# Global attention of a two-layer hybrid block: wider steps for the row maxima, single banks for the scores, values in larger pieces, and another order around them

## The chip, the core and the metric

The kernel runs on one core of a Trainium2 chip. A core has five engines with a queue each: TensorE (PE, matrix products), VectorE (DVE), ScalarE (ACT), GpSimd (POOL) and SyncE (SP, which here only starts DMAs). Each queue takes its instructions in order, and an instruction that waits holds back those behind it. The metric is the device time of one execution in microseconds (us). The profile is one execution taken by the hardware profiler; its times count from the first instruction of the span.

## What is computed

A stack of two layers works on 1024 latent tokens and 256 context tokens of width 1024. Cut to what matters here:

```python
for l in range(2):
    h  = rms_norm(x, norm_gain[l]) * (1 + scale) + shift          # also for ctx
    aq, ak, av, ag, bz, bg, nq, nk, nv, ng = split(h @ w_in[l])
    # global attention: 8 query heads, 2 key heads (4 query heads share one), head size 64
    aq, ak = rope_2d(rms_norm(aq)) * 64**-0.5, rope_2d(rms_norm(ak))
    a_out  = softmax(aq @ concat(ak, ak_ctx).T) @ concat(av, av_ctx)   # 1024 x 1280 per head
    b_out  = pool_branch(bz)                                        # mean windows
    n_out  = neighbourhood_attn(nq, nk, nv, rpb)                    # 8 x 16 windows, plus ctx
    y = concat(a_out * silu(ag), b_out * silu(bg), n_out * silu(ng)) @ w_out[l]
    x = x + gate * y
```

Every value is float32. Where the kernel needs a matrix product of that precision at a higher rate, it splits an operand into a rounded high part and the rest (`hh` and `hl`) and adds the products.

## The kernel before, in words

A layer has the stages input projection, neighbourhood attention (for the first layer also attention of the context tokens over themselves), global attention, and output projection. This change is about the global attention and about the neighbourhood stage ahead of it, in which the first steps of the global attention are hidden.

The **global attention** is cut into eight *units* (`ga_unit`): half of the latent tokens (512 columns, `cc`), one key head `g`, and a pair of query heads, which the code counts with `hi` 0 and 1. In a unit the 1280 keys are taken in five *fifths* (`kp` 0 to 4) of 256 keys. For each fifth and head:

- `scores`: four matmuls of 512 columns on PE into a pair of PSUM banks (1024 columns, `ps_w`, there are two pairs), then one ACT exponential of 1024 columns into a probability buffer `gp` (pool `prob`, seven buffers).
- the sum over keys: the probability tiles of the fifths are added up elementwise in `gacc`, on POOL for fifths 1 to 3 (lines 1037 and 1040) and on DVE for fifth 4, after which DVE folds it to 512 columns (line 1042).
- `values`: the product with the value vectors (line 1049), four matmuls into `ps_c`. It stands one fifth behind the scores.

When a unit is through, ACT copies the product to SBUF (`gosb`), and `finish` follows in the middle of the next unit: PE sums `gacc` over the partitions (line 1058), ACT takes logarithm and exponential (`gr`) for the reciprocal, DVE refines it, POOL multiplies the product with the loaded gate (`ggate`, line 1067), DVE multiplies the two, and `store_u` writes the rounded part (`hh`, ACT) and the rest (`hl`, DVE).

A softmax needs the **maximum of each row** first. `shift` gets it in 20 steps for each unit: PE multiplies 128 queries by 512 keys into one of the three single banks `ps_b` (lines 1003 and 1008), and DVE reduces the bank (`gmx`, lines 1004 and 1009). A 21st step, `shift_rows`, transposes the maxima on PE, ACT copies them (`gmr`), and two small DMAs write them as a row into `q2`, by which the scores come out with the maximum already taken off. These steps run ahead of their unit: 161 closures stand in one list, `shifts`, and `shift_step(n)` takes n of them at each place. Before the first unit starts, 21 + `GA_AHEAD` = 29 of them are to be through; they run in the last 10 (second layer: 7) blocks of the neighbourhood stage, three to a block (one after head 0, two after head 1), what is left at its end.

The **neighbourhood stage** takes 128 queries at a time (`pair_unit`), here called a *block*: two heads, each with scores in a pair of banks, exponential, transposes of the probabilities in two of the three single banks, and the product with the values. The first layer has 28 blocks (20 and 8 of the context), the second 16. What must be loaded or computed early is hung on the block's number with `early(i, fn)`.

PE's order is as the code is written. The order on the other engines is made by the framework's planner, which places each instruction by its own estimate of when it is ready; SP's order too. The order that came out is fixed in the program: the engines don't change it when they run.

Of the kernel before, what the change touches and what calls it, by code (L numbers as in the profile page):

```python
# [31 lines left out]
GA_AHEAD = 8  # L32
# [42 lines left out]
def hybrid_block_kernel(  # L75
# [298 lines left out]
    for l in range(DEPTH):  # L374
# [532 lines left out]
        def early(i, fn):  # L907
            before.setdefault(max(i, 0), []).append(fn)

        order = [0, 1, 6, 7, 4, 5, 2, 3] + list(range(NTL, ntq))  # L910
        for pr in range(2):
# [13 lines left out]
            else:  # L925
                early(s0 + 4, lambda: gk(0))
# [48 lines left out]
        def ga_unit(cc, g, pr):  # L975
# [16 lines left out]
            def shift(i):  # L992

                hi, j = divmod(i, 10)
                if i == 0:
                    load2()
                    st.mx = small.tile([P, 2, 4, 3], F32, tag="gmx", name="gmx")
                q1, mx = st.q1[hi], st.mx[:, hi]
                k1 = gk(g)[0]
                S = ps_one("ps_m")  # L1000
                if j < 8:
                    qt, half = divmod(j, 2)
                    PE.matmul(S, q1[:, qt * P:(qt + 1) * P], k1[:, half * 512:(half + 1) * 512], start=True, stop=True)  # L1003
                    DVE.reduce_max(out=mx[:, qt, half:half + 1], in_=S, axis=AX.X)  # L1004
                    return
                q0 = 2 * (j - 8)
                for i in range(2):
                    PE.matmul(S[:, i * 256:(i + 1) * 256], q1[:, (q0 + i) * P:(q0 + i + 1) * P], k1[:, SEQ:NT], start=True, stop=True)
                DVE.reduce_max(out=mx[:, q0:q0 + 2, 2], in_=S.rearrange("p (a b) -> p a b", a=2), axis=AX.X)
                if hi and j == 9:  # L1010
                    st.nn = small.tile([P, 8], F32, tag="gnn", name="gnn")
                    DVE.tensor_reduce(out=st.nn, in_=st.mx.rearrange("p h q k -> p (h q) k"), op=ALU.max, axis=AX.X, negate=True)
# [11 lines left out]
            def scores(hi, kp):  # L1024
                k1, k2 = gk(g)
                S = ps_pair("ps_st").rearrange("p (a b) -> p a b", a=2)
                for i in range(2):
                    kc = slice((2 * kp + i) * P, (2 * kp + i + 1) * P)
                    PE.matmul(S[:, i, :], k1[:, kc], st.q1[hi], start=True, stop=False)  # L1029
                    PE.matmul(S[:, i, :], k2[:, kc], st.q2[hi], start=False, stop=True)  # L1030
                p = ap_.tile([P, 2, 512], F32, name="gp", tag="prob", bufs=PB)
                ACT.activation(out=p, in_=S, func=AF.Exp)  # L1032
                st.p[hi, kp] = p
                pf = p.rearrange("p a b -> p (a b)")
                if kp == 1:
                    st.acc[hi] = ap_.tile([P, 1024], F32, name="gacc", tag="prob", bufs=PB)
                    POOL.tensor_tensor(out=st.acc[hi], in0=st.p[hi, 0].rearrange("p a b -> p (a b)"), in1=pf, op=ALU.add)  # L1037
                elif kp > 1:
                    eng = DVE if kp == 4 else POOL
                    eng.tensor_tensor(out=st.acc[hi], in0=st.acc[hi], in1=pf, op=ALU.add)  # L1040
# [13 lines left out]

            def finish():
                s_ps = ps_one("ps_gs")
                for hi in range(2):
                    PE.matmul(s_ps[hi * 64:(hi + 1) * 64, :], ones, st.acc[hi][:, 0:512], start=True, stop=True)
                gt = ap_.tile([P, 512], F32, name="ggate", tag="fin", bufs=4)
                SP.dma_start(out=gt, in_=agd[f, :, cs])  # L1060
                r0 = ap_.tile([P, 512], F32, name="gr0", tag="fin", bufs=4)
                ACT.activation(out=r0, in_=s_ps, func=AF.Ln)
                ACT.activation(out=r0, in_=r0, func=AF.Exp, scale=-1.0)
# [3 lines left out]
                POOL.tensor_tensor(out=gt, in0=gt, in1=st.osb, op=ALU.mult)
# [28 lines left out]
        n_shifts = 7 if last else 10  # L1096
        n_ahead = 21 + GA_AHEAD
# [6 lines left out]
        n_all = len(shifts)  # L1104
        for n, u in enumerate(units + [None, None]):
# [4 lines left out]
            for hi in range(2):  # L1110
# [16 lines left out]
        shift_step(n_ahead - (n_all - len(shifts)))  # L1127
# [30 lines left out]
        gunits[-1][2](4, 0)  # L1158
        gunits[-1][2](4, 1)
# [176 lines left out]
```

## Time and profile before

| | |
|---|---|
| median of 3 runs | 1539.0 us (1536.47 to 1542.13) |
| the profiled execution | 1539.72 us, span 1537.9 us |
| granted TensorE clock, mean | 0.996 |
| busy share of the span | PE 96%, DVE 56%, ACT 41%, POOL 33% |
| neighbourhood stage, layer 0 and 1 | about 391 to 513 us, and 1134 to 1227 us |
| global attention, layer 0 and 1 | 513.26 to 730.27 us, and 1226.7 to 1443.74 us |

The page gives for each engine the time in which it was busy, and for groups of like instructions the line, the operation, the output and input tiles, the shapes, the count, the busy time, the mean duration and the idle time of the engine ahead of them with what ended it. In the order of time, a row gives the start, the duration, the engine, the line, the operation, the tiles, the count, and in brackets the idle time ahead of it and what ended it. PE's matmuls overlap: the start of the next row, not the duration, tells how long one holds the engine. A matmul of float32 (line 1049, 1058) shows as two records.

### The profile page before, as it was taken

The page shows a single profiled execution, that of the slowest core. Times are in us where ns is not written, and L with a number is a line of the kernel's source. Part 1 is how long each engine was busy: PE and PEld are TensorE (multiplying, and loading weights), DVE is VectorE, ACT ScalarE, POOL GpSimd, SP SyncE. Part 2 cuts the span into 40 slices and gives each one's busy share as a digit, 9 for nine tenths or more (in the row PEclk, how much of TensorE's full clock was granted, in tenths as well). Part 3 has the DMA queues.
Part 4 walks back from the last instruction along what each step waited for, and adds up shares of the span by engine and source line. Part 5 has one row for each costly group of instructions (what it writes and reads, how often), then busy time and mean ns, then how long its engine had stood idle before and what let it go on. Part 6 is the DMA issues. An engine that isn't in the chain of part 4 may idle for free.

```text
span 1537.9 us, 22259 instructions
## 1 busy us (share of the span) xinstructions
PE 1474.2 (96%) x8001; PEld 1072.8 (70%) x8001; DVE 860.2 (56%) x1666; ACT 637.6 (41%) x1220; POOL 513.1 (33%) x630
## 2 busy tenths in 40 slices
PE   5999999999999999998999999999998999999999
PEld 3787777788888555553788888878787854544577
DVE  3645234552678678875533543464358868786522
ACT  4543132333676444444312452332466544444400
POOL 0232336000134556565001233460013265565300
PEclk9999999999999999999999999999999999999999
DMA  9436455537745200101413222243697301001331
GB/s 317 140 97 219 133 158 162 165 107 192 178 113 159 73 27 25 39 8 55 168 58 109 76 93 91 85 142 82 155 227 172 89 21 42 21 24 39 133 121 55
DMA packets 153039, 167.91 MB, mean 109 GB/s; under 512 B 35384, under 2 KB 112032, under 8 KB 152864
## 3 DMA queue, kind: packets, MB, share of 16 engines
q1 hardware_dynamic: 152928, 166.48, 37.0%
q8 instruction: 63, 1.03, 0.3%
q14 instruction: 48, 0.39, 0.1%
HBM read 126.45 MB, written 40.86 MB: 109 GB/s over the span
## 4 chain that ended last, share of the span: by engine, by line
PE 80%; DVE 8%; ACT 4%; DMA 3%; issue 3%; SPq 1%; POOL 0%; DVEq 0%; POOLq 0%; ACTq 0%
PE ps_w L418 8%; PE ps_w L419 8%; PE ps_w L420 8%; PE ps_c L1049 8%; PE ps_w L1204 4%; PE ps_w L1207 4%; PE ps_w L1205 4%; PE ps_w L1029 4%; PE ps_b L1003 4%; PE ps_w L1030 3%; PE ps_c L894 3%; PE ps_b L882 2%; PE ps_w L426 2%; PE ps_w L428 2%; PE ps_w L427 2%
## 5 line engine op out<-in xcount | busy, mean ns | idle before, releaser
L1032 ACT ACTIVATE gp<-ps_w 128x1024 f32<-128x1024 f32 x160 | 162.4, 1022 | 190.9 <-PE ps_w L1030 155.3
L418 PE MATMUL ps_w<-wh,hh 128*128 128x512 f32 (+1 forms) x624 | 235.7, 378 | 2.2 <-ACT wh L287 2.2
L419 PE MATMUL ps_w<-wl,hh 128*128 128x512 f32 (+1 forms) x624 | 229.0, 367 | 1.0 <-DVE wl L288 1.0
L420 PE MATMUL ps_w<-wh,hl 128*128 128x512 f32 (+1 forms) x624 | 228.4, 366 | 0.0
L1004 DVE TENSOR_REDUCE gmx<-ps_b 128x1 f32<-128x512 f32 x256 | 171.7, 685 | 73.2 <-PE ps_b L1003 69.0
L1049 PE MATMUL ps_c<-gp,av 128*64 128x512 f32 x640 | 165.0, 609 | 10.3 <-ACT gp L1032 10.3
L1040 POOL TENSOR_TENSOR gacc<-gacc,gp 128x1024 f32<-128x1024 f32 x64 | 161.4, 2548 | 25.8 <-ACT gp L1032 25.5
L418 PEld LDWEIGHTS ps_w<-wh,hh 128*128 128x128 f32 x624 | 118.4, 190 | 27.8 <-issue 4.0
L419 PEld LDWEIGHTS ps_w<-wl,hh 128*128 128x128 f32 x624 | 117.8, 189 | 21.3 <-DVE wl L288 2.2
L420 PEld LDWEIGHTS ps_w<-wh,hl 128*128 128x128 f32 x624 | 117.6, 188 | 21.3
L1030 PE MATMUL ps_w<-gq,kst 128*128 128x512 f32 x320 | 126.7, 396 | 0.0
L1204 PE MATMUL ps_w<-woh,hh 128*128 128x512 f32 x272 | 109.5, 403 | 0.0
L1205 PE MATMUL ps_w<-wol,hh 128*128 128x512 f32 x272 | 107.4, 395 | 0.0
L639 DVE TENSOR_REDUCE qss<-sq 128x8 f32<-128x512 f32 (+2 forms) x58 | 31.1, 537 | 135.7 <-ACT sq L637 135.7
L1049 PEld LDWEIGHTS ps_c<-gp,av 128*64 128x64 f32 x640 | 42.5, 136 | 87.3 <-issue 65.2
L1037 POOL TENSOR_TENSOR gacc<-gp 128x1024 f32<-128x1024 f32 x32 | 75.8, 2369 | 50.0 <-ACT gp L1032 50.0
L288 DVE TENSOR_TENSOR wl<-wraw,wh 128x512 fp32r<-128x512 f32 (+1 forms) x96 | 66.3, 707 | 38.8 <-ACT wh L287 37.4
L1207 PE MATMUL ps_w<-woh,hl 128*128 128x512 f32 x272 | 85.6, 395 | 0.0
L426 PE MATMUL ps_w<-hh,wh 128*128 128x512 f32 (+1 forms) x208 | 81.6, 392 | 2.4 <-ACT wh L287 2.4
L866 ACT ACTIVATE prob<-ps_w,m 128x768 f32<-128x768 f32 (+2 forms) x88 | 72.7, 826 | 19.4 <-DVE m L853 7.4
L428 PE MATMUL ps_w<-hh,wl 128*128 128x512 f32 (+1 forms) x208 | 79.6, 382 | 0.0
L427 PE MATMUL ps_w<-hl,wh 128*128 128x512 f32 (+1 forms) x208 | 79.2, 381 | 0.0
(225 smaller groups left out, 2916.2 us busy)
## 6 DMA issues: line engine op xcount, KB each, us to landing
wmod<-in_w_mod_dram SPq DMA_DIRECT2D x48, 512.0 KB
wraw<-in_w_in_dram SPq DMA_DIRECT2D x64, 256.0 KB
gq<-qad SPq DMA_DIRECT2D x64, 128.0 KB
woraw<-in_w_out_dram SPq DMA_DIRECT2D x14, 512.0 KB
wraw<-in_w_in_dram SPq DMA_DIRECT2D x48, 128.0 KB
kst<-knd SPq DMA_DIRECT2D x16, 320.0 KB
qad<-qkhi SPq DMA_DIRECT2D x18, 256.0 KB
qad<-qklo SPq DMA_DIRECT2D x18, 256.0 KB
```

Of the source, the lines that this page charges most:

```text
L418: PE.matmul(ps[:, :n], a, wh[:, off:off + n], start=(k == 0), stop=False)
L419: PE.matmul(ps[:, :n], a, wl[:, off:off + n], start=False, stop=False)
L420: PE.matmul(ps[:, :n], b, wh[:, off:off + n], start=False, stop=(k == KT - 1))
L426: PE.matmul(ps[:, :n], wh[:, fs], hh[:, k, ts_], start=(k == 0), stop=False)
L1004: DVE.reduce_max(out=mx[:, qt, half:half + 1], in_=S, axis=AX.X)
L1030: PE.matmul(S[:, i, :], k2[:, kc], st.q2[hi], start=False, stop=True)
L1032: ACT.activation(out=p, in_=S, func=AF.Exp)
L1040: eng.tensor_tensor(out=st.acc[hi], in0=st.acc[hi], in1=pf, op=ALU.add)
L1049: PE.matmul(st.o[hi * 64:(hi + 1) * 64, :], av[:, kt, g * 64:(g + 1) * 64], st.p[hi, kp][:, i, :], start=(kt == 0), stop=(kt == NTT - 1))
L1204: PE.matmul(ps[:, i2, :], a, oh[:, cs], start=(k == 0), stop=False)
L1205: PE.matmul(ps[:, i2, :], a, ol[:, cs], start=False, stop=False)
L1207: PE.matmul(ps[:, i2, :], b, oh[:, i2 * 512:(i2 + 1) * 512], start=False, stop=(k == KT - 1))
```

## The change

- **Maxima.** For the first unit and for head 0 of the second the steps stay as they were (20 and 10 steps, single banks `ps_b`). For all others a step (`shift2`) covers 1024 columns in a pair of banks `ps_w`: 5 steps for a head, each with two matmuls of 512 columns (or four of 256) and one DVE reduction of 1024. The negated maximum is taken for each head by itself (`shift_head`).
- **Scores** go to the three single banks `ps_b`, with one exponential of 512 columns for each bank: two for a fifth and head in place of one.
- **Values** are taken two fifths at a time, at fifth 2 and fifth 4; the last fifth comes at fifth 1 of the next unit, and right behind it the sums (`sums`) and `finish`.
- **The sum over keys** lies in memory of its own (the neighbourhood's values `nv`, and two key buffers), no longer in the ring of probability buffers. In the last unit, head 0's additions run on DVE.
- **Finish.** ACT copies the sums to SBUF; the last product runs on POOL, and ACT's rounded part (`Identity`, line 1095) and DVE's rest (line 1096) are taken from it.
- **Steps ahead.** `GA_AHEAD` is 31 and counts all of them: 30 steps of the old kind and one transpose are through before the first unit; they run in the last 16 blocks of the neighbourhood stage, one after each head. The loads of the first two units' queries and of the first key head move up to the block ahead of that; in the second layer, with 16 blocks, to block 0. In the stage itself there are three steps at a unit's first fifth and two at each of the others.

Three places on which the change acts, in the order in which each engine's instructions stand. The names carry buffer numbers, to tell buffers of one kind apart.

**ACT in unit 1 of layer 0, around the sums of unit 0.** Before; `gp_5981` belongs to head 1 of fifth 2, `gp_6010` and `gp_6032` to the two heads of fifth 3:

```order
L1032 ACTIVATE gp_5981<-ps_w1_3846 128x1024
L1062 ACTIVATE gr0_5996<-ps_b1_70 128x512
L1063 ACTIVATE gr0_5996<-gr0_5996 128x512
L1032 ACTIVATE gp_6010<-ps_w0_3845 128x1024
L1032 ACTIVATE gp_6032<-ps_w1_3846 128x1024
L815 ACTIVATE hh_95<-gt1_5999 128x512
L1019 ACTIVATE gmr_6036<-ps_b1_70 8x128
```

After; `gp_5971` belongs to head 1 of fifth 1, `gp_5985` and `gp_6006` to the two heads of fifth 2:

```order
L1074 ACTIVATE gosb_5954<-ps_c_72 128x512
L1081 ACTIVATE gr0_5958<-ps_b0_69 128x512
L1082 ACTIVATE gt1_5959<-ps_b0_69 128x512
L1088 ACTIVATE gr0_5958<-gr0_5958 128x512
L1053 ACTIVATE gp_5971<-ps_b1_70 128x512
L1053 ACTIVATE gp_5971<-ps_b2_71 128x512
L1053 ACTIVATE gp_5985<-ps_b0_69 128x512
L1053 ACTIVATE gp_5985<-ps_b1_70 128x512
L1095 ACTIVATE hh_95<-ggate_5962 128x512
L1053 ACTIVATE gp_6006<-ps_b2_71 128x512
L1053 ACTIVATE gp_6006<-ps_b0_69 128x512
```

The rounded part for `hh` stands four exponentials of 512 columns behind the sums, with the exponentials of head 1 of fifth 2 right behind it; before, it stood two of 1024 behind.

**POOL in the same unit.** Before:

```order
L1067 TENSOR_TENSOR ggate_5994<-ggate_5994,gosb_5919 128x512
L1037 TENSOR_TENSOR gacc_5940<-gp_5910,gp_5938 128x1024
L1037 TENSOR_TENSOR gacc_5956<-gp_5928,gp_5954 128x1024
L1040 TENSOR_TENSOR gacc_5940<-gacc_5940,gp_5966 128x1024
L1040 TENSOR_TENSOR gacc_5956<-gacc_5956,gp_5981 128x1024
```

After:

```order
L1058 TENSOR_TENSOR gacc_5755<-gp_5910,gp_5939 128x1024
L1058 TENSOR_TENSOR gacc_5756<-gp_5926,gp_5971 128x1024
L1091 TENSOR_TENSOR ggate_5962<-ggate_5962,gosb_5954 128x512
L1061 TENSOR_TENSOR gacc_5755<-gacc_5755,gp_5985 128x1024
L1093 TENSOR_TENSOR ggate_5962<-ggate_5962,gt1_5959 128x512
L1061 TENSOR_TENSOR gacc_5756<-gacc_5756,gp_6006 128x1024
```

Before, the product with the gate stood ahead of the unit's additions; now it stands between them, and the second product (line 1093), which writes what `hh` is taken from, stands behind the addition for head 0 of fifth 2.

**PE at the start of layer 1's neighbourhood stage.** `kst_10615` is the rounded part of key head 0 of the global attention. Before:

```order
L428 MATMUL ps_c_72<-hh_95,wl_10257 128x512
L846 MATMUL ps_w0_10531<-kst_10348,nq_10360 128x256
L847 MATMUL ps_w0_10531<-kst_10349,nq_10360 128x256
...
L882 MATMUL ps_b1_70<-ident_85,prob_10593 128x128 x4
```

After:

```order
L428 MATMUL ps_c_72<-hh_95,wl_10274 128x512
L1001 MATMUL ps_b1_70<-kst_10615,hh_95 128x512
L1001 MATMUL ps_b2_71<-kst_10615,hh_95 128x512
L846 MATMUL ps_w1_10549<-kst_10365,nq_10377 128x256
L847 MATMUL ps_w1_10549<-kst_10366,nq_10377 128x256
...
L882 MATMUL ps_b0_69<-ident_85,prob_10625 128x128 x4
```

The first two steps of the maxima stand between the last matmul of the gate projection and the first scores of the stage. On SP, the key head's load stands behind the loads of two units' queries:

```order
L372 DMA hh_95<-qad_77 64x512 x2
L730 DMA agd_81<-gate_10537 128x512
L372 DMA hl_96<-qad_77 64x512 x2
L372 DMA hh_95<-qad_77 64x512 x2
L372 DMA hl_96<-qad_77 64x512 x2
L755 DMA kst_10615<-kad_78 64x1280 x2
```

Before, three loads of queries stood there; the other five came later in the stage's first blocks, and the key head's load was hung on block 12 of 16.

The diff, cut to its core:

```diff
-GA_AHEAD = 8
+GA_AHEAD = 31
...
-                early(s0 + 4, lambda: gk(0))
+                pass
...
+            def shift_head(hi, n):
+                DVE.tensor_reduce(out=st.nn[:, 4 * hi:4 * hi + 4], in_=st.mx[:, hi, :, 0:n], op=ALU.max, axis=AX.X, negate=True)
...
+            def shift2(hi, j):
+                if j == 0:
+                    (load2 if hi else shift_new)()
+                S = ps_pair("ps_m")
+                if j < 4:
+                    for half in range(2):
+                        shift_mm(hi, S, j, half * 512, half * 512, 512)
+                    DVE.reduce_max(out=st.mx[:, hi, j, 0:1], in_=S, axis=AX.X)
+                    return
+                for qt in range(4):
+                    shift_mm(hi, S, qt, qt * 256, SEQ, 256)
+                DVE.reduce_max(out=st.mx[:, hi, :, 1], in_=S.rearrange("p (a b) -> p a b", a=4), axis=AX.X)
+                shift_head(hi, 2)
...
             def scores(hi, kp):
                 k1, k2 = gk(g)
-                S = ps_pair("ps_st").rearrange("p (a b) -> p a b", a=2)
+                p = ap_.tile([P, 2, 512], F32, name="gp", tag="prob", bufs=PB)
                 for i in range(2):
+                    S = ps_one("ps_st")
                     kc = slice((2 * kp + i) * P, (2 * kp + i + 1) * P)
...
-                p = ap_.tile([P, 2, 512], F32, name="gp", tag="prob", bufs=PB)
-                ACT.activation(out=p, in_=S, func=AF.Exp)
+                    PE.matmul(S, k1[:, kc], st.q1[hi], start=True, stop=False)
+                    PE.matmul(S, k2[:, kc], st.q2[hi], start=False, stop=True)
+                    ACT.activation(out=p[:, i, :], in_=S, func=AF.Exp)
...
-                    st.acc[hi] = ap_.tile([P, 1024], F32, name="gacc", tag="prob", bufs=PB)
+                    st.acc[hi] = accs[n % 2][hi]
...
-                    eng = DVE if kp == 4 else POOL
+                    eng = DVE if kp == 4 or (n == 7 and hi == 0) else POOL
...
+            def sums():
+                S = ps_one("ps_gs")
+                for hi in range(2):
+                    PE.matmul(S[hi * 64:(hi + 1) * 64, :], ones, st.acc[hi][:, 0:512], start=True, stop=True)
...
+                ACT.activation(out=st.r0, in_=S, func=AF.Ln)
+                ACT.activation(out=st.t1, in_=S, func=AF.Copy)
+
             def finish():
...
-                DVE.tensor_tensor(out=t1, in0=s_ps, in1=r0, op=ALU.mult)
+                DVE.tensor_tensor(out=t1, in0=t1, in1=r0, op=ALU.mult)
                 DVE.scalar_tensor_tensor(out=t1, in0=t1, scalar=-2.0, in1=r0, op0=ALU.add, op1=ALU.mult)
                 POOL.tensor_tensor(out=gt, in0=gt, in1=st.osb, op=ALU.mult)
-                DVE.scalar_tensor_tensor(out=t1, in0=t1, scalar=-1.0, in1=gt, op0=ALU.mult, op1=ALU.mult)
-                store_u(f, cc * 512, 512, t1)
...
+                POOL.tensor_tensor(out=gt, in0=gt, in1=t1, op=ALU.mult)
+                hi, lo = hh[:, f, cs], hl[:, f, cs]
+                ACT.activation(out=hi, in_=gt, func=AF.Identity, scale=-1.0)
+                DVE.scalar_tensor_tensor(out=lo, in0=gt, scalar=-1.0, in1=hi.bitcast(F32), op0=ALU.mult, op1=ALU.subtract)
...
+                way, k = (0, 10) if i + hi < 2 and i < 2 else (6, 5)
...
+        n_shifts = min(len(units), (GA_AHEAD + 1) // 2)
         for i in range(2):
-            early(len(units) - 12, gunits[i][4])
+            early(len(units) - n_shifts - 1, gunits[i][4])
+        early(len(units) - n_shifts, lambda: gk(0))
...
-                if hi == 0 and n >= nun - n_shifts:
-                    shift_step(1, n_all - n_ahead)
-            shift_step(2 if n >= nun - n_shifts else 0, n_all - n_ahead)
+                if n >= nun - n_shifts:
+                    shift_step(1, n_least)
...
             for kp in range(5):
-                lagv = None
-                if kp:
-                    lagv = lambda h, kp=kp: values(kp - 1, h)
-                elif pv:
-                    lagv = lambda h: pv[2](4, h)
                 scores(0, kp)
                 shift_step(1)
-                if lagv:
-                    lagv(0)
-                    lagv(1)
-                shift_step(2 if kp == 4 else 1)
+
+                if kp == 1 and pv:
+                    pv[2](4, 0)
+                    pv[2](4, 1)
+                    pv[7]()
+                    pv[3]()
+                elif kp in (2, 4):
+                    for j in range(4):
+                        values(kp - 2 + j // 2, j % 2)
                 scores(1, kp)
-                shift_step(2)
-                if kp == 2 and pv:
-                    pv[3]()
+                shift_step(2 if kp == 0 else 1)
```

In these loops `u[4]` is `load`, `pv[7]` is `sums`, `pv[3]` is `finish`, and `way` 0 and 6 are `shift` and `shift2`.

More of the change, by code (lines that the diff above doesn't have):

```diff
@@ L990, in load2, with shift_new, shift_mm, shift @@
                     load_parts(st.q2[hi], qad, 2 * f + hi, cs)
[L992 to L999, printed above, removed]
+            def shift_new():
+                st.mx = small.tile([P, 2, 4, 3], F32, tag="gmx", name="gmx")
+                st.nn = small.tile([P, 8], F32, tag="gnn", name="gnn")
+            def shift_head(hi, n):
+                DVE.tensor_reduce(out=st.nn[:, 4 * hi:4 * hi + 4], in_=st.mx[:, hi, :, 0:n], op=ALU.max, axis=AX.X, negate=True)
+            def shift_mm(hi, S, qt, o, k0, n):
+                PE.matmul(S[:, o:o + n], st.q1[hi][:, qt * P:(qt + 1) * P], gk(g)[0][:, k0:k0 + n], start=True, stop=True)
+            def shift(hi, j):
+                if j == 0:
+                    (load2 if hi else shift_new)()
                 S = ps_one("ps_m")
@@ L1002, in shift @@
                     qt, half = divmod(j, 2)
-                    PE.matmul(S, q1[:, qt * P:(qt + 1) * P], k1[:, half * 512:(half + 1) * 512], start=True, stop=True)
-                    DVE.reduce_max(out=mx[:, qt, half:half + 1], in_=S, axis=AX.X)
+                    shift_mm(hi, S, qt, 0, half * 512, 512)
+                    DVE.reduce_max(out=st.mx[:, hi, qt, half:half + 1], in_=S, axis=AX.X)
                     return
@@ L1007, in shift @@
                 for i in range(2):
[L1008 to L1012, printed above, removed]
+                    shift_mm(hi, S, q0 + i, i * 256, SEQ, 256)
+                DVE.reduce_max(out=st.mx[:, hi, q0:q0 + 2, 2], in_=S.rearrange("p (a b) -> p a b", a=2), axis=AX.X)
+                if j == 9:
+                    shift_head(hi, 3)
+            def shift2(hi, j):
+                if j == 0:
+                    (load2 if hi else shift_new)()
+                S = ps_pair("ps_m")
[8 more added lines that the diff above has]
+                shift_head(hi, 2)
             def shift_rows():
@@ L1055, in finish @@
             def finish():
-                s_ps = ps_one("ps_gs")
-                for hi in range(2):
-                    PE.matmul(s_ps[hi * 64:(hi + 1) * 64, :], ones, st.acc[hi][:, 0:512], start=True, stop=True)
                 gt = ap_.tile([P, 512], F32, name="ggate", tag="fin", bufs=4)
                 SP.dma_start(out=gt, in_=agd[f, :, cs])
-                r0 = ap_.tile([P, 512], F32, name="gr0", tag="fin", bufs=4)
-                ACT.activation(out=r0, in_=s_ps, func=AF.Ln)
+                r0, t1 = st.r0, st.t1
@@ L1075, in hybrid_block_kernel @@
+            return shift, scores, values, finish, load, shift_rows, shift2, sums
+        gunits = [ga_unit(4 * cc + 2 * g + pr, cc, g, pr) for cc in range(2) for g in range(2) for pr in range(2)]
         shifts = []
         for i, u in enumerate(gunits):
-            own = [lambda u=u, j=j: u[0](j) for j in range(20)]
+            own = []
+            for hi in range(2):
+                way, k = (0, 10) if i + hi < 2 and i < 2 else (6, 5)
+                own += [lambda u=u, way=way, hi=hi, j=j: u[way](hi, j) for j in range(k)]
@@ L1136, in hybrid_block_kernel @@
         nu = len(gunits)
+        nvf = nv.rearrange("p t c -> p (t c)")
+        accs = [[nvf[:, 0:1024], nvf[:, 1024:2048]],
+                [ak_.tile([P, NT], F32, name="gacc", tag="kst", bufs=6)[:, 0:1024] for _ in range(2)]]
         for i in range(nu):
-            _, scores, values, finish, _, _ = gunits[i]
+            _, scores, values, finish = gunits[i][:4]
             pv = gunits[i - 1] if i else None
```

18 lines of the change are left out of this document (6 added, 12 removed).

## Prediction

> **What bounds the kernel now.** I read the chain of waits first. Its first line says that four fifths of the time to the end hang on PE. The table of windows with the two global attention stages comes next (the last three columns are PE's granted clock, the DMA share and GB/s), and then PE's waits in the first stage (us in total, times, longest).
>
> ```profile
> PE 80%; DVE 8%; ACT 4%; DMA 3%; issue 3%; SPq 1%; POOL 0%; DVEq 0%; POOLq 0%; ACTq 0%
> 513.26:730.27 217.01, 205.37 (x841) 106.82 (x840) 156.12 (x200) 98.68 (x116) 128.86 (x59) 0.99 0.10 30
> 1226.70:1443.74 217.04, 205.46 (x840) 106.72 (x839) 157.03 (x201) 98.70 (x116) 128.80 (x58) 0.99 0.10 31
> PE ps_b L1003 <- DVE gmx L1004: 6.4, 6, 1.2
> PE ps_c L1049 <- ACT gp L1032: 5.1, 3, 3.1
> ```
>
> The stages are alike, so one is worked out and doubled. PE (first pair) is busy 205 of 217 us; DVE, ACT and POOL have 60 to 118 us of slack each, but POOL's 129 us come in few, long pieces. PE waits 11.5 us in nine places. That is the most that better timing alone can win in a layer.
>
> Then PE's order of time for a steady unit, with the starts of units 4 and 6 (617.48, 671.71), the end of 6 and the end of 7:
>
> ```profile
> 605.05 1.08 PE L1058 MATMUL ps_b<-gacc,ones 128*64 128x512 f32 x4
> 606.06 0.50 PE L1029 MATMUL ps_w<-hh,kst 128*128 128x512 f32 x1
> 617.14 0.50 PE L1003 MATMUL ps_b<-kst,hh 128*128 128x512 f32 x1 [1.24 <-DVE gmx L1004]
> 617.48 0.40 PE L1029 MATMUL ps_w<-hh,kst 128*128 128x512 f32 x1
> 617.71 0.40 PE L1030 MATMUL ps_w<-gq,kst 128*128 128x512 f32 x1
> 618.41 0.44 PE L1008 MATMUL ps_b<-kst,hh 128*128 128x256 f32 x2
> 618.78 1.94 PE L1049 MATMUL ps_c<-gp,av 128*64 128x512 f32 x8
> 620.64 0.50 PE L1008 MATMUL ps_b<-kst,hh 128*128 128x256 f32 x2
> 671.71 0.40 PE L1029 MATMUL ps_w<-hh,kst 128*128 128x512 f32 x1
> 698.41 0.39 PE L1029 MATMUL ps_w<-hh,kst 128*128 128x512 f32 x1
> 730.27 0.50 PE L1204 MATMUL ps_w<-woh,hh 128*128 128x512 f32 x1
> ```
>
> A unit takes (671.71 - 617.48)/2 = 27.11 us, unit 6 26.70, unit 7 31.86. A matmul of 512 columns holds PE for 0.23 us (617.48 to 617.71; 0.2325 over longer rows), the values of a fifth for 1.86 (618.78 to 620.64), the sums for 1.01. Where PE goes from 128-column to 64-column weights, a step lasts longer than its matmuls (618.41 to 618.78 is 0.37, two of 256 columns); I put 0.2 on each group of values or sums. A unit is then 40 matmuls of scores 9.3, five fifths of values 9.3, sums 1.0, 20 steps of maxima 4.65, six groups at 0.2: 25.5, and one stall of 1.24 where DVE hasn't emptied a single bank. That makes 26.7 of 27.11.
>
> **The change in the steady units.** *Removed:* three of the six groups per unit, 0.6 us, so 24.9 of work. The maxima's matmuls stay as many. The pair of banks for the scores goes, and the accumulators leave the ring of probability buffers. *Added and moved:* I followed the new orders by hand, with durations from these rows (groups: count | busy, mean ns), and ACT's rows in order of time:
>
> ```profile
> L1040 POOL TENSOR_TENSOR gacc<-gacc,gp 128x1024 f32<-128x1024 f32 x64 | 161.4, 2548 | 25.8 <-ACT gp L1032 25.5 <-ACT gmr L1019 0.2
> L1037 POOL TENSOR_TENSOR gacc<-gp 128x1024 f32<-128x1024 f32 x32 | 75.8, 2369 | 50.0 <-ACT gp L1032 50.0
> L1067 POOL TENSOR_TENSOR ggate<-ggate,gosb 128x512 f32<-128x512 f32 x16 | 20.6, 1290 | 99.9 <-ACT gosb L1053 93.3 <-DVE gmx L1009 6.6
> L1004 DVE TENSOR_REDUCE gmx<-ps_b 128x1 f32<-128x512 f32 x256 | 171.7, 685 | 73.2 <-PE ps_b L1003 69.0
> L1262 DVE TENSOR_TENSOR yg<-ps_w,gateb 128x1024 f32<-128x1024 f32 x17 | 20.8, 1222 | 78.0 <-PE ps_w L1207 77.8
> 606.18 0.60 ACT L1062 ACTIVATE gr<-ps_b 128x512 f32<-128x512 f32 x1 [0.41 <-PE ps_b L1058]
> 606.81 0.63 ACT L1063 ACTIVATE gr<-gr 128x512 f32<-128x512 f32 x1
> 607.34 1.01 ACT L1032 ACTIVATE gp<-ps_w 128x1024 f32<-128x1024 f32 x1
> ```
>
> ACT takes 512 columns every 0.53 to 0.63 us. Exponentials of 512 have no row; 0.53 each (half of 1.01 would be the low end, 0.63 the high). Let T be the moment when PE is through the sums of the unit before.
>
> *ACT and POOL:* logarithm, copy and exponential of the sums occupy ACT to T+1.9. The exponentials of head 1 of fifth 1 end at T+3.0, those of head 0 of fifth 2 at T+4.0. Next on ACT stands the rounded part of `hh`, which waits for POOL. POOL's order is: first addition for head 1, product with the gate, addition for head 0 of fifth 2, second product. The first addition needs both exponentials of head 1, so from T+3.0 that is 2.5 + 1.3 + 2.5 + 1.3 us, to T+10.6. The rounded part ends at T+11.2, and only then come the exponentials of head 1 of fifth 2, the first at T+11.8. DVE's refinement isn't late (done by T+6).
>
> *PE meanwhile:* two scores of head 1 (0.93), a step of maxima (0.47), head 0 of fifth 2 (0.93, with a wait of 0.6 for the first exponential of head 1), a step (0.47), two fifths of values (3.9), head 1 of fifth 2 (0.93), a step (0.47), half of head 0 of fifth 3 (0.47). At T+9.2 it wants the third bank back, and that holds head 1 of fifth 2, whose exponential ends at T+11.8. So PE stands 2.6 us, the values that follow with it. Behind it another 0.45 for the next bank.
>
> *Maxima:* one reduction of 1024 columns has no row. DVE's 1024 columns out of PSUM with a multiplication take 1.22 us, two reductions of 512 take 1.37; half that, 0.69, would be the floor. I take 1.2, since the kind of reading is that of the first row. At a unit's start three steps come within 2 us, with a 1024-column addition, a fold and two more reductions ahead on DVE: by hand the two pairs make PE wait 1.25 and 0.35, in place of today's 1.24. With 0.7 both waits would go.
>
> So a steady unit is 24.9 + 0.6 + 2.6 + 0.45 + 1.6 = 30.1, **3.0 more**; five of them are +15. Unit 0 has no finish behind it: 0. Unit 6 has five steps of maxima fewer (2.3), some of which goes back into the hold: 28.5, +1.8.
>
> *Unit 7:* two stalls in units 6 and 7 are the ring of buffers: ACT waits for POOL's additions. After the second the clock falls:
>
> ```profile
> 695.51 1.93 PE L1049 MATMUL ps_c<-gp,av 128*64 128x512 f32 x6 [1.88 <-ACT gp L1032]
> 721.39 1.12 PE L1049 MATMUL ps_c<-gp,av 128*64 128x512 f32 x4 [3.08 <-ACT gp L1032]
> 695.50:698.41 2.91, 2.90 (x10) 1.33 (x11) 1.93 (x1) 0.87 (x1) 2.37 (x1) 1.00 0.27 106
> 721.40:728.10 6.70, 6.53 (x16) 2.24 (x18) 4.08 (x3) 1.88 (x2) 2.35 (x1) 0.75 0.16 37
> ```
>
> The accumulators no longer take two of the seven buffers and head 0's additions run on DVE, so by hand nothing there waits as long as 0.5 us: 31.86 loses 3.08, a quarter of 6.7 (1.7) and 0.6 of groups: 26.5, **-5.4**. Per layer +15 + 1.8 - 5.4 = +11.4, for both **+22.8**.
>
> **The neighbourhood stage and the first steps.** PE's waits for single banks in this stage, two rows of layer 0 and three of layer 1:
>
> ```profile
> PE ps_b L1003 <- DVE gmx L1004: 1.2, 3, 0.6
> PE ps_b L1003 <- DVE gmx L1009: 0.7, 2, 0.3
> PE ps_b L1008 <- ACT probt L887: 1.3, 1, 1.3
> PE ps_b L1003 <- ACT probt L887: 1.2, 5, 0.4
> PE ps_b L1003 <- DVE gmx L1004: 0.8, 1, 0.8
> ```
>
> These 5.2 us come mostly where two steps stand back to back. One step after each head lets most of that go; two steps more per layer (0.34 each, as from 617.14 to 617.48) cost some 1.4. I take -3 for both layers, bounds -5 and +4. In layer 1 the stage has 16 blocks, so its first two steps now stand on PE right behind the last gate projection:
>
> ```profile
> 1133.57 0.40 PE L428 MATMUL ps_c<-hh,wl 128*128 128x512 f32 x1
> 1137.50 0.33 PE L882 MATMUL ps_b<-ident,rg 128*128 128x128 f32 x1 [0.78 <-POOL rg L869]
> 1127.67 1.19 SPq L372 DMA_DIRECT2D hh<-qad x2
> 1129.64 0.33 SPq L730 DMA_DIRECT2D agd<-gate x1
> hh<-qad SPq DMA_DIRECT2D x32, 128.0 KB
> kst<-kad SPq DMA_DIRECT2D x12, 320.0 KB
> 1126.74:1137.50 10.76, 9.95 (x61) 8.72 (x61) 5.50 (x15) 6.81 (x14) 0.68 (x3) 1.00 0.91 240
> ```
>
> They are due at 1133.8 and need the key head. On SP its two loads (320 KB each) stand behind two loads of queries, the store at 1129.64 and six more loads of 128 KB at 0.55 to 0.6 each: issued by about 1134.5. From 1127.67 that is 1.0 + 0.26 + 0.64 MB, at the window's 240 GB/s 7.9 us, to 1135.6 at the earliest; with what is under way at 91% and what follows an issue, 1137 to 1142. PE, with scores queued behind, stands some 5 us; the clock falls (1.7), today's wait of 0.78 is covered: **+6**, bounds 2 and 11. In layer 0 the key head comes blocks ahead of its use: 0.
>
> Sum: 22.8 - 3 + 6 = +25.8. The profiled execution (1539.72) and its span (1537.9) would become 1565.5 and 1563.7. The median of the runs shown is 1539.0, 0.7 below the profiled one: **1565 us**. Its own range is 1553 to 1577, from the bounds of the neighbourhood stage and 0.3 us either way on the 12 holds.
>
> **Rivals.** *The hold doesn't bite (faster).* It decides between PE's wish at T+9.2 and POOL's second product at T+10.6: were POOL's two additions 1.3 us each shorter, or the exponentials of head 1 ahead of the rounded part, PE wouldn't stop. Against it: 96 additions average 2.4 to 2.5, and the order is fixed. For it: these are averages with DVE's operations beside them, and a wait of 2.6 rests on a sum of ten durations. Without the 3.6 us of hold a steady unit is 26.5 (-0.6), unit 6 25.7 (-1.0): a layer -9.4, both -18.8, with -3 + 6 about -16: 1523. With the maxima's waits gone too, -1.6 in six units of both layers: 1504. *Half the hold*, POOL quicker by 1.3 in all: 1.3 less in 12 units, 1549. *The clock falls at each hold.* A stop of 1.88 left it at 1.00 and one of 3.08 brought 0.75 for 6.7 us; 2.6 lies between. Then 12 times 1.7: 1585. [...]
>
> **Chances.** Forecast 0.50, clock falls 0.18, half the hold 0.12, hold doesn't bite 0.20. The 12 us to either side of 1565 carry the forecast; the range goes to 1512 and 1588 and leaves out a third of the faster case and the end of the clock case. A measurement of this kernel tells about 0.5% (7.7 us) from no change: 1531 to 1547. Faster takes most of the last case, 0.19; same the lower end of half the hold, 0.08; slower 0.73.
>
> **What would show it.** In the profile after: PE's waits headed by scores (`ps_b`) on ACT, some 2.6 us six times per layer, and ACT idle 6 to 7 us ahead of the rounded part (line 1095) for POOL's product (line 1093); steady units near 30; no stall over 1 us in unit 7 and its clock at 1.00; PE standing at the start of layer 1's neighbourhood stage for the key head. It is wrong if ACT's idle time there is under 4 us, if units take under 27, or if the window of the first global stage isn't near 228 us.

## The result: slower by 2.8%, and the profile after

The changed kernel takes 1580.85 us (median of 4 runs, 1577.57 to 1584.7) against 1537.74 for the kernel before in the same comparison: a ratio of 1.0277 (1.0244 to 1.0311). That is 43 us where 26 were forecast. The profiled execution takes 1579.93 us with a span of 1578.1, which is 40.2 more than before.

The first line of the chain of waits, then the windows of the two global attention stages and of the two neighbourhood stages, these from the end of the gate projection on (PE, PEld, DVE, ACT, POOL busy; then PE's granted clock):

```profile
PE 75%; DVE 11%; DMA 4%; ACT 3%; issue 3%; POOL 2%; SPq 1%; DVEq 0%; ACTq 0%; POOLq 0%
508.53:747.83 239.30, 211.15 (x837) 111.97 (x835) 158.85 (x134) 106.36 (x203) 132.51 (x64) 0.94 0.09 28
1244.11:1482.62 238.51, 210.36 (x838) 110.72 (x836) 159.67 (x134) 105.65 (x203) 132.36 (x63) 0.94 0.10 30
394.89:508.53 113.64, 109.12 (x1063) 93.85 (x1061) 92.43 (x256) 82.50 (x197) 46.01 (x131) 1.00 0.59 154
1150.06:1244.11 94.05, 85.37 (x859) 77.77 (x858) 75.42 (x193) 60.07 (x121) 24.70 (x73) 0.96 0.60 146
```

The same windows of the neighbourhood stages before:

```profile
398.96:513.26 114.30, 108.86 (x1059) 93.57 (x1057) 91.78 (x252) 82.86 (x197) 42.76 (x129) 1.00 0.59 154
1133.80:1226.75 92.95, 85.84 (x854) 75.86 (x853) 74.92 (x190) 60.01 (x121) 28.14 (x76) 1.00 0.62 149
```

All of the loss lies in the global attention: 239.3 and 238.5 us against 217.0 twice, 43.8 us, with the clock at 0.94 where it was 0.99. The neighbourhood stages changed by -0.7 and +1.1. Before the first of them 4.1 us were gained, which can't be put down to the change: experiments 3 and 11 below, whose edits lie behind that point, come there 0.1 and 3.9 us ahead of the kernel before.

Where it goes in a stage shows in PE's waits of the first one, and in PE's rows around one of them (583.37) with the starts of units 1 and 6 (530.84, 690.36):

```profile
PE ps_b L1051 <- ACT gp L1053: 18.7, 7, 3.5
PE ps_w L1001 <- DVE gmx L1028: 5.2, 6, 0.9
PE ps_b L1038 <- DVE gnn L998: 2.9, 1, 2.9
530.84 0.40 PE L1051 MATMUL ps_b<-hh,kst 128*128 128x512 f32 x1
579.74 0.40 PE L1052 MATMUL ps_b<-gq,kst 128*128 128x512 f32 x1
583.37 0.80 PE L1051 MATMUL ps_b<-hh,kst 128*128 128x512 f32 x1 [3.23 <-ACT gp L1053]
585.46 0.63 PE L1051 MATMUL ps_b<-hl,kst 128*128 128x512 f32 x1
585.89 0.63 PE L1052 MATMUL ps_b<-gq,kst 128*128 128x512 f32 x1
589.58 3.65 PE L1070 MATMUL ps_c<-gp,av 128*64 128x512 f32 x16
690.36 0.40 PE L1051 MATMUL ps_b<-hh,kst 128*128 128x512 f32 x1
```

Seven waits for ACT's exponentials, 3.2 to 3.5 us each in the steady units, where waits for ACT came to 5.1 us in the whole stage before. After the stop a matmul of 512 columns holds PE for 0.43 us (585.46 to 585.89) and not 0.23, until 589.58: the clock has fallen (granted 0.55 from 585.46 to 589.58). Units 1 to 5 take (690.36 - 530.84)/5 = 31.90 us, 4.8 more than before. Two windows of 10 us behind such stops show the most and the least of the fall in this stage:

```profile
583.30:593.30 10.00, 9.93 (x32) 5.52 (x33) 5.67 (x6) 4.13 (x9) 7.02 (x3) 0.71 0.09 27
647.60:657.60 10.00, 10.00 (x39) 5.74 (x40) 6.82 (x6) 4.65 (x10) 7.04 (x3) 0.85 0.10 27
```

That is 1.5 to 2.9 us lost behind each stop. The cause of the stop, on ACT, POOL and DVE in the same unit (the sums end on PE at T = 571.04):

```profile
582.21 0.63 ACT L1095 ACTIVATE hh<-ggate 128x512 fp32r<-128x512 f32 x1 [7.50 <-POOL ggate L1093]
573.81 2.38 POOL L1058 TENSOR_TENSOR nv<-gp 128x1024 f32<-128x1024 f32 x1 [3.08 <-ACT gp L1053]
576.14 1.72 POOL L1091 TENSOR_TENSOR ggate<-ggate,gosb 128x512 f32<-128x512 f32 x1
577.83 2.40 POOL L1061 TENSOR_TENSOR nv<-nv,gp 128x1024 f32<-128x1024 f32 x1
580.91 1.26 POOL L1093 TENSOR_TENSOR ggate<-ggate,gt 128x512 f32<-128x512 f32 x1 [0.69 <-DVE gt L1090]
573.89 2.85 DVE L1089 TENSOR_TENSOR gt<-gt,gr 128x512 f32<-128x512 f32 x1
577.86 2.91 DVE L1090 SCALAR_TENSOR_TENSOR gt<-gt,gr 128x512 f32<-128x512 f32 x1
```

ACT stands 7.5 us at the rounded part, with the exponentials that PE needs behind it. POOL's four operations come in the order that was forecast and near its pace (the product with the gate takes 1.72 us, not 1.3); one thing is new: POOL itself waits 0.69 us for DVE. DVE's two products take 2.85 and 2.91 us. Each begins with a POOL addition under way and ends some 0.55 us behind it (576.74 behind 576.19, 580.77 behind 580.23).

### The profile page after: what moved, and what is told of

Same layout as the page of the kernel before. It is cut to its first block, busy times and chain, and to the rows that moved or that the text cites. A ratio compares the mean times of both kernels' runs of the same rounds, so it can differ in the third digit from the quotient of the medians.

```text
span 1578.1 us, 22314 instructions
## 1 busy us (share of the span) xinstructions
PE 1480.1 (94%) x8001; PEld 1081.1 (69%) x8001; DVE 869.7 (55%) x1540; ACT 653.5 (41%) x1396; POOL 523.8 (33%) x642
## 4 chain that ended last, share of the span: by engine, by line
PE 75%; DVE 11%; DMA 4%; ACT 3%; issue 3%; POOL 2%; SPq 1%; DVEq 0%; ACTq 0%; POOLq 0%
PE ps_w L418 8%; PE ps_w L419 8%; PE ps_w L420 8%; PE ps_c L1070 6%; PE ps_w L1236 4%; PE ps_w L1238 4%; PE ps_w L1235 4%; PE ps_b L1051 4%; PE ps_c L894 3%; PE ps_b L1052 3%; PE ps_b L882 3%; PE ps_w L1001 3%; PE ps_w L426 2%; PE ps_w L428 2%; PE ps_w L427 2%
## 5 line engine op out<-in xcount | busy, mean ns | idle before, releaser
L1053 ACT ACTIVATE gp<-ps_b 128x512 f32<-128x512 f32 x320 | 171.7, 600 | 135.9 <-PE ps_b L1052 135.6
L1070 PE MATMUL ps_c<-gp,av 128*64 128x512 f32 x640 | 152.7, 614 | 0.0
L1028 DVE TENSOR_REDUCE gmx<-ps_w 128x1 f32<-128x1024 f32 x104 | 124.3, 1218 | 44.9 <-PE ps_w L1001 44.9
L1052 PE MATMUL ps_b<-gq,kst 128*128 128x512 f32 x320 | 135.0, 422 | 0.0
L1051 PE MATMUL ps_b<-hh,kst 128*128 128x512 f32 x160 | 71.2, 445 | 38.8 <-ACT gp L1053 37.1
L1061 POOL TENSOR_TENSOR nv<-nv,gp 128x1024 f32<-128x1024 f32 x32 | 76.2, 2402 | 14.9 <-ACT gp L1053 14.9
L637 ACT ACTIVATE sq<-ps_w 128x512 f32<-128x512 f32 (+2 forms) x58 | 27.9, 481 | 123.4 <-PE ps_w L420 123.4
```

The source lines that it names most:

```text
L1028: DVE.reduce_max(out=st.mx[:, hi, j, 0:1], in_=S, axis=AX.X)
L1051: PE.matmul(S, k1[:, kc], st.q1[hi], start=True, stop=False)
L1052: PE.matmul(S, k2[:, kc], st.q2[hi], start=False, stop=True)
L1053: ACT.activation(out=p[:, i, :], in_=S, func=AF.Exp)
L1070: PE.matmul(st.o[hi * 64:(hi + 1) * 64, :], av[:, kt, g * 64:(g + 1) * 64], st.p[hi, kp][:, i, :], start=(kt == 0), stop=(kt == NTT - 1))
```

## The experiments

Experiments 3, 10 and 11 edit the kernel before, the others the changed kernel. Each is compared with the kernel before on the same chip (1537.8 to 1539.0 us there); the change itself has the ratio 1.0277.

**1. The rounded part on POOL.** `ACT.activation(out=hi, ...)` of line 1095 becomes `POOL.tensor_scalar(out=hi, in0=gt, scalar1=-1.0, ...)`.

> The changed kernel with one edit: the rounded part of `hh` (line 1095) runs on POOL, right behind the product that it is taken from, so that ACT's exponentials no longer stand behind it. Theory (ACT waits there for POOL, PE for ACT, and PE's clock falls for the stop): in the changed kernel seven stops of 2.0 to 3.2 us per layer come to 21 us, and the mean clock of a stage is 0.94 of 239 us, some 14 us. Both go: 35 us per layer, 70 in all, less a few for POOL's one more operation (1.2 us per unit): 1511 to 1525 us, units of 26 to 27 us, PE's wait for ACT's exponentials under 8 us in all, stage clock 0.99 or more. Rival A (the clock has another cause): only the stops go, 42 us, 1539, clock still 0.94. Rival B (another queue holds PE as long at the same place): over 1560.

Measured: 1607.96 us, ratio 1.0452 (1.0430 to 1.0475), slower than the change. ACT's waits went, and a longer stop came at the same fifth, for DVE:

```profile
554.99 2.82 DVE L1096 SCALAR_TENSOR_TENSOR hl<-ggate,hh 128x512 fp32r<-128x512 f32 x1 [3.05 <-POOL hh L1095]
559.00 1.22 PE L1001 MATMUL ps_w<-kst,hh 128*128 128x512 f32 x2 [4.38 <-DVE gmx L1028]
```

DVE's queue stood for the same chain: the rest `hl` waits for `hh`, and the maxima's reductions stand behind it. Taking one of two queues out of a chain that both wait for, while the chain gets some 3 us longer, costs: on POOL the rounded part took 1.50 us, not 0.63, and the rest beside POOL's additions 2.82, not 0.69. Rival B held; it was a queue that the theory hadn't named.

**2. The sums read from PSUM.** Line 1082 is taken out, and DVE reads the bank.

```diff
-                ACT.activation(out=st.t1, in_=S, func=AF.Copy)
-                DVE.tensor_tensor(out=t1, in0=t1, in1=r0, op=ALU.mult)
+                DVE.tensor_tensor(out=t1, in0=st.s, in1=r0, op=ALU.mult)
```

> The changed kernel without ACT's copy of the sums (line 1082): DVE's first product reads the sums from PSUM, as before the change. The order of POOL comes out other by one place: the second product now stands ahead of the addition for head 0 of fifth 2. Theory: that takes 2.4 us of addition out of the chain that ends in the rounded part: addition 2.4, product 1.7, product 1.3 from T+2.8 is T+8.2, rounded part T+8.8, exponential T+9.4, against PE's wish near T+9. The stop shrinks from 3.2 to under 1 us, and with no long stop the clock stays up: 1515 to 1530. DVE's first product falls from 2300 ns to about 690 (one input in PSUM). Rival A (clock falls have another cause): stops gone, clock 0.94: 1540 to 1550. Rival B: DVE's product stays above 2000 ns, so its pace isn't a matter of where its input lies.

Measured: 1555.54 us, ratio 1.0112 (1.0093 to 1.0131), better than the change and short of the 1515 to 1530 of the theory. DVE's first product by groups, in the changed kernel and in this one, then one of the new stops, the windows of 10 us behind it and behind the next one, and the stage:

```profile
L1089 DVE TENSOR_TENSOR gt<-gt,gr 128x512 f32<-128x512 f32 x16 | 36.8, 2302 | 12.7 <-ACT gr L1088 12.7
```

```profile
L1089 DVE TENSOR_TENSOR gt<-ps_b,gr 128x512 f32<-128x512 f32 x16 | 10.9, 684 | 12.4 <-ACT gr L1088 12.4
574.02 0.50 PE L1051 MATMUL ps_b<-hh,kst 128*128 128x512 f32 x1 [1.91 <-DVE gt L1089]
574.02:584.02 10.00, 9.88 (x42) 5.55 (x43) 6.61 (x6) 5.11 (x10) 9.48 (x6) 1.00 0.00 0
602.61:612.61 10.00, 9.89 (x35) 4.89 (x35) 6.46 (x5) 4.01 (x8) 7.87 (x5) 0.83 0.00 0
510.64:733.55 222.91, 202.61 (x838) 106.80 (x836) 158.41 (x134) 104.05 (x196) 132.53 (x64) 0.98 0.10 30
```

With one input in PSUM the product takes 684 ns, not 2302. The stop for ACT is gone as expected; the faster product and POOL's other order, which came with the edit, aren't told apart in this. But the sums' bank is now held until DVE gets to it, 1.9 us, which wasn't foreseen. The clock is 0.98: behind the stop at 574.02 it stays at 1.00, behind the one at 602.61, as long, it falls to 0.83. Of the twelve such stops in both layers seven were followed by a fall.

**3. The accumulators' memory, and head 0's additions of the last unit on DVE**, in the kernel before:

```diff
-                    st.acc[hi] = ap_.tile([P, 1024], F32, name="gacc", tag="prob", bufs=PB)
+                    st.acc[hi] = accs[n % 2][hi]
-                    eng = DVE if kp == 4 else POOL
+                    eng = DVE if kp == 4 or (n == 7 and hi == 0) else POOL
```

> The kernel before with one part of the change alone: the sums over keys lie in memory of their own (and head 0's additions of the last unit run on DVE). Theory (the stalls of 1.9 and 3.1 us at the end of each stage come from the ring of probability buffers): both and the fall of the clock behind the second go, 6.7 us per layer, 13 in all: 1522 to 1529. Rival (POOL's pace sets them, with any buffers): under 4 us, 1534 or more.

Measured: 1529.35 us, ratio 0.9938 (0.9922 to 0.9954): faster than both kernels. The stage, and all of PE's waits in it:

```profile
513.12:724.50 211.38, 204.41 (x841) 106.64 (x839) 156.16 (x202) 98.69 (x116) 122.66 (x57) 1.00 0.10 31
PE ps_b L1003 <- DVE gmx L1004: 4.8, 6, 0.9
PE ps_c L1049 <- ACT gp L1032: 1.0, 1, 1.0
PE ps_b L1058 <- DVE gacc L1042: 0.7, 1, 0.7
```

The stage is 5.6 us shorter, and its clock stays at 1.00. Of the waits, ACT's fell by 4.1 us: in unit 6 from 1.88 to 1.02, in unit 7 from 3.08 to nothing. In unit 6 only the memory differs, so that part was the ring's; in unit 7 the additions on DVE may have helped, and the run doesn't tell the two apart. Another 1.6 us came from shorter waits for the maxima in the steady units (1.24 to 0.91 each), which the theory hadn't named.

**4. Layer 1's first steps three blocks later** (`n_shifts = min(len(units) - 3, ...)`).

> The changed kernel, with the first steps of the maxima of layer 1 (and the loads that they need) starting three blocks later, and six steps left for the end of the stage. Theory: PE's stop of 5.8 us at the stage's start for the key head goes, and the fall of the clock behind it (about 1.7); six steps at the end cost some 2.5: a gain of 3 to 6, 1575 to 1578. Rival (the loads are late wherever they stand, or the block's other loads wait as long): no change, 1580 or more.

Measured: 1582.6 us, ratio 1.0285 (1.0264 to 1.0305), no gain: the rival held. The loads hang on the block ahead of the first step, so they moved with it, and PE waited 4.92 us for the key head at the later place.

**5. The gate loaded early.** `ggate`'s load moves from `finish` to the start of the unit.

> The changed kernel with one edit: the gate of a unit's finish is loaded at the start of the next unit. In POOL's order the product with the gate then stands ahead of head 1's first addition instead of behind it. Theory A (POOL's order alone makes the rounded part late): 1.7 us leave the chain between T+2.8 and the second product, which ends near T+9.4, the stop shrinks from 3.2 to about 1.6 us, the clock stays up: 1535 to 1550. Theory B (DVE's two products, 2.8 and 2.9 us each where POOL adds beside them, end at T+9.7 and hold POOL's second product): the stop stays near 3 us: 1575 to 1583.

Measured: 1567.54 us, ratio 1.0178 (1.0156 to 1.0199), between the two theories. One of PE's stops and the stage:

```profile
582.35 0.51 PE L1051 MATMUL ps_b<-hh,kst 128*128 128x512 f32 x1 [1.98 <-ACT gp L1053]
510.86:739.39 228.53, 207.47 (x838) 109.14 (x836) 155.96 (x134) 105.26 (x203) 132.63 (x64) 0.96 0.10 29
```

The stop shrinks by 1.25 of the 1.7 us that left POOL's chain: POOL's order sets much of it. POOL's second product still waits 0.69 us for DVE, as in the changed kernel. The clock is 0.96, lower than in experiment 2 with stops hardly longer: here nine of the ten stops of 2.0 us in both layers were followed by a fall.

**6. Sums and finish at fifth 2**, behind the values of two fifths.

> The changed kernel with the sums and the finish moved from a unit's fifth 1 to its fifth 2, behind the values of two fifths. In ACT's order the rounded part then stands behind the exponentials of head 0 of fifth 4, where PE has 3.7 us of values ahead. Theory (what costs is that ACT and DVE stand for the rounded part while PE has only 9 us of work that doesn't need them): the chain of 11 us now ends about when PE is through those values; stops under 1 us, the clock at 0.98 or more, units of 27 to 28 us: 1520 to 1545. Rival (the chain's length costs wherever it stands, through DVE's queue or the banks): stops over 2 us, 1565 or more.

Measured: 1589.93 us, ratio 1.0325 (1.0307 to 1.0343). PE's waits for ACT fall to 1.3 us at most, and stops of 2.1 and 1.6 come at the next unit's start, for DVE's reductions. The rival held.

**7. The rounded part and the rest both on POOL** (`store_u(f, cc * 512, 512, gt, POOL)`).

> The changed kernel with both the rounded part and the rest on POOL, so that neither ACT's exponentials nor DVE's reductions stand behind them (with the rounded part alone on POOL, PE stopped 4.4 us for DVE, whose `hl` waited). Theory (the cost is two queues that stand for the end of the finish): no stop over 1.3 us in a steady unit, clock 0.99: units 26 to 27 us, 1510 to 1528. Rival (POOL, with 20 of 26 us of work, becomes late with the additions, and PE waits for DVE's last addition at the sums): 1545 or more.

Measured: 1592.06 us, ratio 1.0346 (1.0331 to 1.0360). The middle of the unit is free of stops, as the theory said, and the rival decides: POOL's additions end late, DVE waits for them with its last addition, and PE for the reductions behind it.

```profile
558.66 3.40 DVE L1061 TENSOR_TENSOR gacc<-gacc,gp 128x1024 f32<-128x1024 f32 x1 [3.78 <-POOL gacc L1061]
563.98 0.73 PE L1001 MATMUL ps_w<-kst,hl 128*128 128x512 f32 x2 [2.88 <-DVE gmx L1032]
566.32 1.22 PE L1001 MATMUL ps_w<-kst,hl 128*128 128x512 f32 x2 [1.60 <-DVE gmx L1028]
```

**8. Both reliefs together:** experiment 7, with experiment 5's early gate and head 0's addition at fifth 3 on DVE:

```diff
-                    eng = DVE if kp == 4 or (n == 7 and hi == 0) else POOL
+                    eng = DVE if kp == 4 or (hi == 0 and (kp == 3 or n == 7)) else POOL
```

> The changed kernel with three edits: the finish's rounded part and rest both on POOL, its gate loaded at the start of the unit, and head 0's addition at fifth 3 on DVE in place of POOL. Theory (two causes in turn: ACT and DVE stand for the end of the finish; and with that away, POOL's three additions come 20 us after the sums, DVE's last addition waits for them with the maxima's reductions behind it): without head 0's addition POOL's last one ends near T+17.7, before the exponential that DVE's last addition needs (T+18.5); stops of PE under 1.3 us, stage clock 0.99 or more, stages of 203 to 212 us: 1508 to 1530. Rival (DVE's additions with POOL beside them, up to 3.4 us each, make the reductions late all the same): stops over 2 us at the start of a unit, 1550 or more.

Measured: 1537.18 us, ratio 0.9995 (0.9984 to 1.0005): the 43 us are gone, and no gain is left. The stage and the stops of a steady unit (units 27.66 us, 564.54 to 592.20):

```profile
510.76:725.85 215.09, 200.49 (x838) 104.42 (x836) 170.29 (x134) 101.52 (x196) 141.27 (x71) 0.99 0.11 33
564.54 0.74 PE L1001 MATMUL ps_w<-kst,hl 128*128 128x512 f32 x2 [1.60 <-DVE gmx L1028]
592.20 0.73 PE L1001 MATMUL ps_w<-kst,hl 128*128 128x512 f32 x2 [1.60 <-DVE gmx L1028]
```

Less the stop a unit takes 26.06 us. The unit before, less its 1.24, takes 25.87. What PE does between the stops took no less time in the new order.

**9. The same, with layer 1's loads three to four blocks ahead of the first steps.**

> The kernel of e11_relief, with layer 1's loads for the first steps of the maxima three to four blocks ahead of the steps, which start at block 4. Theory (PE's stop of 5 us for the key head is load time that four blocks cover): the stop goes, seven steps are left for the stage's end (some 3 us): 1 to 5 us under e11_relief. Rival (the stage's other waits take up what the stop gives, as they gave back 4.6 us of it in the changed kernel): within 1 us of e11_relief.

Measured: 1535.25 us, ratio 0.9988 (0.9977 to 1.0000). The stop for the key head went, and another came for a gate, whose load now stands behind the key head's:

```profile
1131.15 0.58 SPq L834 DMA_DIRECT2D ngate<-ngd  x1
1138.27 0.61 POOL L869 TENSOR_SCALAR rg<-ngate,rr 128x64 f32<-128x64 f32 x2 [5.34 <-DMA ngate<-ngd]
1138.93 0.47 PE L882 MATMUL ps_b<-ident,rg 128*128 128x128 f32 x1 [4.63 <-POOL rg L869]
1127.52:1221.39 93.87, 87.68 (x858) 78.59 (x856) 75.21 (x193) 60.33 (x121) 29.92 (x77) 0.96 0.62 150
```

The neighbourhood stage gained 2.0 us (95.9 in experiment 8); the medians differ by 1.9 in the same direction, but their intervals overlap, so the whole time doesn't tell the theory from the rival.

**10. Experiment 3 with layer 0's first steps spread as in the change**, its loads earlier.

> The kernel before with two parts of the change: the sums over keys in memory of their own (1529.4 us by itself), and in the first layer alone the first steps of the maxima one after each head in the last 16 blocks, with their loads earlier. Theory (the first layer's neighbourhood stage got 4.7 us shorter in the changed kernel by this): 1523 to 1526. Rival (that gain came with other parts): 1528 to 1531.

Measured: 1531.62 us, ratio 0.9952 (0.9939 to 0.9966). The neighbourhood stage became 1.0 us shorter, the global stage behind it 3.4 longer (214.8 against 211.4): PE's waits in it grew by 2.9 us, and the one for a bank in each unit is 1.23 in place of 0.91. The steps now stand at other places of the unit; that this is the reason wasn't tested by itself. The gain of the theory didn't come.

**11. Experiment 3 with one step of the maxima moved from fifth 4 to fifth 2.**

> The kernel of e3_acc_own (1529.4 us), with one step of the maxima less at the end of a unit's fifth 4 and one more in its fifth 2. Theory (what is left of stops in a steady unit, 0.91 us, comes from the steps that follow each other there while DVE is at its additions and folds): the stop goes, some 0.9 us in ten units: 1519 to 1524. Rival (the place of the steps only moves the wait, as it did in e9_acc_spread, where it grew from 0.91 to 1.23): 1528 to 1535.

Measured: 1529.35 us, ratio 0.9939 (0.9924 to 0.9954), the same as experiment 3: the rival held. The wait of 0.91 went, waits of 0.3 and 0.2 came at two other places of each unit and one of 1.0 in unit 6, and the stage became 0.8 us shorter (210.6).

## Why the prediction was right, and where it was not

**The place and the cause were right.** The forecast's sentence that PE stands because ACT waits at the rounded part for POOL is what the profile shows, row by row, and experiments 1, 2, 5, 7 and 8 each change the chain and move the stop.

**The case was the rival's.** The forecast of 1565 left the clock at 1.00; the third rival, the clock falling at each hold, gave 1585. It fell at the holds, by 1.5 to 2.9 us each. The price of 1.7 per stop was near, and the two stages' +43.8 is what that rival had: 22.8 + 12 x 1.7 = 43.2. By the forecast's own sign, a first global stage not near 228 us, its central case was wrong: that stage took 239.3. The time lies in the stated range because the range was drawn to take in part of this rival. That the sum came so near is partly luck: in a steady unit the work was 1.2 us too low, and the waits beside the hold 1.5 too high.

**The steady unit**, 30.1 forecast and 31.90 measured:

- *The work, 24.9, was 1.2 too low.* "Three of the six groups per unit, 0.6 us" was the failed step: a unit less its stop took 25.87 before and 26.06 in experiment 8. The groups did get shorter there: values and sums take 9.9 us, 10.3 before. But pauses that the list of waits leaves out took that up: two matmuls hold PE for 0.46 and 0.52 us in place of 0.23, and the transpose of the maxima with the matmul behind it 0.72, 0.35 before. The 0.4 us by which the sum had missed the old unit should also have been carried on.
- *The hold, 2.6, measured 3.23.* "DVE's refinement isn't late (done by T+6)" failed, and no row stood beside it: DVE's second product ended at T+9.73, and POOL's second product waited 0.69 us for it, which is about the difference. The copy of the sums made both inputs of DVE's first product lie in SBUF, where it ended 0.55 us behind POOL's addition and took 2.85 us (its row stands in the section on the result). The row of the profile before that could have told it is that of the old last product, `L1068`, with a mean of 2086 ns.
- *The waits of 0.6 and 0.45* beside it measured 0.3 at most. *The maxima's waits*, 1.6, measured 0.85: a reduction of 1024 columns took 1.22 us, as estimated.
- *The clock*, nothing forecast, about 2.1 (mean of five windows).

That is 26.1 + 3.2 + 0.85 + 2.1 = 32.2, against 31.90.

**Units 6 and 7**, 28.5 + 26.5 forecast, 57.5 measured (690.36 to 747.83). That the ring's stalls would go was right; that experiment 3 measures 5.6 us against the -5.4 is partly luck, since 1.6 of them came from other waits. In unit 6 PE stood 2.9 us for the maxima (`L998`, behind DVE's first product of 2.81 us) in place of the hold for ACT. In unit 7, where no stall over 1 us and a clock of 1.00 had been forecast, it stood 2.0 us for ACT, and the clock was 0.83 in the 10 us behind each of the two.

**The neighbourhood stages.** The stop for the key head was right (5 forecast):

```profile
1155.99 1.19 PE L1001 MATMUL ps_b<-kst,hh 128*128 128x512 f32 x2 [5.76 <-DMA kst<-kad]
```

The stage still grew by 1.1 us only, since waits of 6.9 us in it before became 2.9 beside the stop. In layer 0 the stage got 0.7 us shorter, not 1.5.

**The rival on the other side**, no hold and 1523 or 1504, would have needed more than a shorter chain: in experiments 1, 6 and 7 the stop went from its place and came back at another, and with most of it relieved in experiment 8 the kernel is at 1537. DVE and POOL, not ACT's queue alone, bound the new order.

## What to carry to other kernels

An instruction that waits holds its whole queue, as ACT's did here for 7.50 us with PE's exponentials behind it; when one is put into a queue that a faster engine depends on, follow every queue that waits for the same chain, since relieving one of them may only show the next. Price an operation with the place of its inputs, not only its size: the same 128x512 product took 684 ns here with an input in PSUM, and 2302 on average with both in SBUF. And take the part of a change that has a measured stall of its own to remove: here the accumulators' own memory, with the last unit's additions on DVE, gave 0.6%, and the rest of the change took back more than that.

## What the runs showed of the hardware

- **DVE's product with both inputs in SBUF ended behind POOL's addition.** The same 128x512 product took 684 ns with one input in PSUM (mean of experiment 2) and 2302 with both in SBUF (mean of the changed kernel): 2.81 to 2.85 us in the twelve of sixteen that ran beside a POOL addition, 0.69 in the four that didn't. Experiment 2 shows both kinds beside one POOL addition:

```profile
572.95 2.37 POOL L1058 TENSOR_TENSOR nv<-gp 128x1024 f32<-128x1024 f32 x1 [2.82 <-ACT gp L1053]
573.29 0.68 DVE L1089 TENSOR_TENSOR gt<-ps_b,gr 128x512 f32<-128x512 f32 x1
574.00 1.87 DVE L1090 SCALAR_TENSOR_TENSOR gt<-gt,gr 128x512 f32<-128x512 f32 x1
```

The product with an input in PSUM runs through while POOL adds; the next one, with both inputs in SBUF, ends at 575.87, 0.55 us behind the addition (575.32), as in the changed kernel. In these rows the two took turns; by what, no trace here shows. POOL's product with the gate took longer too: 1.72 us in the changed kernel, where it starts while such a DVE product is under way, and 1.29 in experiment 5, where none is.

- **The clock fell after short stops, and not after each of the same length.** Over the 10 us behind a stop, the clock stayed at 1.00 behind all ten stops of 1.6 us in experiment 8; it fell to 0.83 behind seven of twelve of 1.9 (experiment 2) and nine of ten of 2.0 (experiment 5), and to 0.70 to 0.85 behind all ten of 3.2 to 3.5 in the changed kernel's steady units. Before the change one of 1.88 passed at 1.00, in the changed kernel's unit 7 one of 2.01 was followed by 0.83 (layer 0) and one of 2.00 by 1.00 (layer 1), and in experiment 4 even one of ten of 3.2 to 3.5 did. A single length doesn't divide them. What else decides it, no run here shows.
